# Class scores of a dilated attention: two classes in one contraction, and zero blocks shared

## Chip, cores and metric

The kernel runs on one core of a Trainium2 chip. The metric is the device time of one execution in microseconds; the time before is the median of three runs. Engines are named as in the profile: PE is TensorE's matmul, PEld its weight load, DVE VectorE, ACT ScalarE, POOL GpSimd, SP the engine that issues most of the DMAs.

## What is computed

One encoder block on a sequence of 1024 positions with 1024 channels, in float32: a normalised input is projected to two token mixers and two gates; the mixers are merged by the gates, projected and added to the input; a squared-ReLU MLP and a last norm follow. The part that matters here is the first mixer, attention of 8 heads of 64 dims over three dilations:

```python
DILATED_PATTERNS = ((128, 1), (512, 4), (2048, 16))
def dilated_window_attention(q, k, v):
    for window, dil in DILATED_PATTERNS:
        half = window // (2 * dil)          # 64 in each
        ...                                 # phase split of the sequence by dil, |i-j| <= half in each phase
        outs.append(o); lses.append(lse)
    w = softmax(stack(lses), axis=0)        # the three outputs weighted by their denominators
    return einsum('pbsh,pbshd->bshd', w, stack(outs))
```

The second mixer (4 heads) is a differential attention over all keys; its result goes through `w_branch_b`, times a gate ("branch B" below).

## The kernel before, in words

Positions are kept by class: position t = 4 m + c lies in class c (4 classes) at m (256 places), so dilation 4 and 16 are products inside one class, and dilation 1 is a product of nearby keys of all classes. Float32 operands are split into a high and a low half (`F32R`), and a product is made of several matmuls on halves.

The stages follow each other in the trace: projections and rotary (`rope`, to about 430 us), the differential attention (to about 650 us), the dilated attention with branch B's products as filling (to about 868 us), output projections, MLP. Pools of tiles are opened and closed with the stages, so a stage's first loads need space that the one before gives up. The order of instructions on each engine is worked out when the kernel is built, by a scheduler that goes by the order of the program text and its own estimate of times; engines then run their lists in order.

In `rope`, tile j < 8 holds two heads of the first mixer (queries j < 4, keys 4 to 7). The rotated tile `raw` is split by an ACT copy and a DVE subtract; for j < 4 these write the halves in tile order (8 tiles of 128 queries, each 4 classes x 32). The halves are stored by DMAs on ACT's queue into `qk_d`.

A unit of the dilated stage is one head h and one tile n of 128 queries; 64 units in a row, with values two units (`LAGA`) behind scores. `a_open` loads a head's tiles: `qs` (queries: 64 dims high, 64 dims low on the 128 partitions), `kh` and `kl` (each half of the keys twice, above and below). `a_scores` makes one bank of 128 x 512: class scores in columns 0 to 255 and local scores in 256 to 511. For the class scores each class c has its own weights in `zq`: the queries of the tile with every column outside class c set to zero, so that the four products add up in one 128 x 256 area:

```python
for c in range(NCLS):
    for kk in (o.kh, o.kl):
        nc.tensor.matmul(ps[:, 0:CM], zq[:, n % 4, c, :], kk[:, c * CM:(c + 1) * CM],
```

Eight matmuls, with (high + low) queries on the partitions against high, then low keys. `zq` is filled by one DVE copy for four tiles. Then DVE adds the mask and finds the minimum, ACT takes the exponential, PE transposes, ACT and DVE write the two halves of the transposed weights into `pta` (ten blocks of 128 for each pair of units, two of them zero), and `a_local` and `a_class` multiply by values. After every second head `a_merge` loads shifted sums (`sh`) and denominators (`zr`) from DRAM, POOL adds and multiplies, and `a_split` makes halves on ACT and DVE.

Branch B's products (`branch_b`, 32 steps) are spread over the units as filling; their operand `obT` is loaded by `load_ob`, its weights by `split_weight` (load, ACT copy, POOL subtract; three buffers).

Of the kernel before, what the change touches and what calls it, by code (L numbers as in the profile page):

```python
# [83 lines left out]
def tile_hybrid_block(ctx: ExitStack, tc: tile.TileContext, t: dict, out: bass.AP):  # L84
# [92 lines left out]
    qk_d = [dram(f"qk{j}", [2, P, S]) for j in range(16)]  # L177
    va_d = [dram(f"va{g}", [S, 4, P]) for g in range(2)]
# [309 lines left out]
    def rope(j, raw):  # L488
# [9 lines left out]
        if j < 4:  # L498

            src, to_hi, to_lo = [x.rearrange("p (a b j) -> p a b j", a=a, j=32) for x, a in ((raw, NCLS), (hi, NT), (lo, NT))]  # L500
            to_hi, to_lo = [x.rearrange("p n c j -> p c n j") for x in (to_hi, to_lo)]
        else:
            src, to_hi, to_lo = raw, hi, lo
        nc.scalar.activation(to_hi, src, AF.Copy)
        nc.vector.tensor_tensor(to_lo, src, f(to_hi), op=ALU.subtract)
# [280 lines left out]
    def strided(x, offset, *dims):  # L786

        a = x[:, 0:1]
        return bass.AP(tensor=a.tensor, offset=a.offset + offset, ap=[list(a.ap[0])] + [list(d) for d in dims])
# [29 lines left out]
    def a_values(o, n):  # L819
# [5 lines left out]
        view = [strided(z, 10 * P * pr + P * x, ((4 + 2 * x) * P, 2), (2 * P, 2), (1, P)) for z in pta]  # L825
# [11 lines left out]
    def a_local(o, pr):  # L837
# [13 lines left out]
    def a_class(o):  # L851
        for g in range(2):
            acc = bank1(f"oc{o.h}_{g}", "mm")
            for c in (2 * g, 2 * g + 1):
                oo = acc[:, (c % 2) * CM:(c % 2 + 1) * CM]
                for z in range(2):
                    for kt in range(2):
                        nc.tensor.matmul(oo, o.vc[:, 2 * c + kt, :],
                                         strided(pta[z], 2 * P * kt + 32 * c, (10 * P, 4), (P, 2), (1, 32)),
# [35 lines left out]
    def branch_b():  # L895
        for cp in range(4):
            wh, wl = split_weight(f"wb{cp}", [P, 4, 256],
                                  [(None, w_b[:, 256 * cp:256 * cp + 256].rearrange("(k p) n -> p k n", p=P))], lo="p")
            for u in range(2):
                j = 2 * cp + u  # L900
                c = slice(P * u, P * u + P)
                for h in range(2):
# [3 lines left out]
                    for k in range(4):  # L906
                        for w, z in ((wh, 0), (wh, 1), (wl, 0)):
                            nc.tensor.matmul(acc, w[:, k, c], obT[z][:, k, 512 * h:512 * h + 512],
                                             start=k == 0 and w is wh and z == 0, stop=k == 3 and w is wl)
# [52 lines left out]
    obT = [pob.tile([P, 4, S], F32R, tag=f"ob{z}", name=f"obT{z}") for z in range(2)]  # L962

    def load_ob(j):
        for z in range(2):
            nc.sync.dma_start(f(obT[z])[:, j, :], ob_d[j][z])

    for j in range(3):
        load_ob(j)
# [5 lines left out]
    zqs = [p2a.tile([P, 4, NCLS, P], F32R, tag=f"zq{n}", name=f"zq{n}") for n in range(2)]  # L975


    pta = [p2a.tile([P, 4, 10, P], F32R, tag=f"pta{z}", name=f"pta{z}") for z in range(2)]
    for x in zqs:
        nc.vector.memset(f(x), 0.0)  # L980
    for z in range(2):
        for b in (5, 8):
            nc.gpsimd.memset(f(pta[z])[:, :, b, :], 0.0)
# [6 lines left out]

    LAGA = 2
    for u in range(8 * AH + LAGA):
        h, n = u // 8, u % 8
        if n == 0 and 0 < h < AH - 1:
            ah[h + 1] = a_open(h + 1)
        if h < AH:
# [5 lines left out]
        if u == 7:  # L1002
            load_ob(3)
# [466 lines left out]
```

## Time and profile before

| | |
|---|---|
| median of 3 runs | 1673.32 us (1667.09 to 1675.45) |
| the profiled execution, its own time | 1674.86 us |
| its span, first to last instruction | 1673.1 us |
| mean granted TensorE clock | 0.972 |
| dilated stage, about | 656 to 866 us |

The span is what the trace covers. In a row of the timeline the first number is the start in us from the span's start, the second the duration; in brackets stands how long the engine was idle before and what ended it. Line numbers (L803) are those of the kernel.

### The profile page before, as it was taken

The numbers are of one execution on the slowest core, as the hardware profiler recorded it, in microseconds if no ns is written. First come the engines' busy times: TensorE is split into PE (matmuls) and PEld (weight loads), VectorE is DVE, ScalarE is ACT, GpSimd is POOL, SyncE is SP. The second block draws the span as 40 slices with busy tenths as digits, with TensorE's granted clock in tenths as the row PEclk, the third lists the DMA queues.
The fourth block names the chain that finished last, engine by engine and source line by source line (L and its number), as shares of the span: only waits on it lengthen the run. The fifth ranks groups of instructions, "written<-read, shape, count | busy, mean of one in ns | idle before, by whom it ended". The sixth has DMA issues, their size and how long they took to land. (4 is left out here: it accounts for less than half of the span.)

```text
span 1673.1 us, 20932 instructions
## 1 busy us (share of the span) xinstructions
PE 1557.9 (93%) x7832; PEld 1299.2 (78%) x7832; DVE 1181.4 (71%) x1367; ACT 697.6 (42%) x1064; POOL 585.3 (35%) x289
## 2 busy tenths in 40 slices
PE   8899889988789998989999999899999989999998
PEld 6798667766577887988887878687888867888776
DVE  5976798698688996645547357644355599898984
ACT  4432122232467774544433236444444552333331
POOL 1534444555232332012220003533333344354551
PEclk8999899998999999999999999999999999999999
DMA  6367566555767557656557333444333571423112
GB/s 214 125 210 215 164 196 223 175 184 163 263 194 233 200 191 271 204 180 215 156 162 278 110 130 94 120 128 130 114 101 101 179 268 51 163 74 116 51 38 101
DMA packets 214389, 271.23 MB, mean 162 GB/s; under 512 B 12784, under 2 KB 136848, under 8 KB 214288
## 3 DMA queue, kind: packets, MB, share of 16 engines
q1 hardware_dynamic: 200464, 236.33, 44.4%
q10 hardware_dynamic: 13824, 33.56, 5.3%
q8 instruction: 62, 1.02, 0.3%
q14 instruction: 39, 0.32, 0.1%
HBM read 183.81 MB, written 80.27 MB: 158 GB/s over the span
## 5 line engine op out<-in xcount | busy, mean ns | idle before, releaser
L1359 PE MATMUL p<-b,a 128*128 128x512 f32 x392 | 154.7, 395 | 5.1 <-DVE b L1274 5.1
L1358 PE MATMUL p<-b,a 128*128 128x512 f32 x392 | 154.2, 393 | 3.0 <-ACT a L1273 3.0
L1360 PE MATMUL p<-b,a 128*128 128x512 f32 x392 | 154.4, 396 | 2.0 <-DVE a L1274 1.9
L1274 POOL TENSOR_TENSOR b<-ws,b 128x1024 fp32r<-128x1024 f32 x20 | 61.4, 3088 | 95.3 <-ACT b L1273 85.3
L1359 PEld LDWEIGHTS p<-b,a 128*128 128x128 f32 x392 | 74.2, 189 | 23.0 <-DVE b L1274 6.0
L1274 POOL TENSOR_TENSOR b<-rb,b 128x1024 fp32r<-128x1024 f32 x21 | 70.8, 3390 | 54.7 <-ACT b L1273 46.7
L1360 PEld LDWEIGHTS p<-b,a 128*128 128x128 f32 x392 | 74.0, 189 | 20.1 <-DVE a L1274 3.9
L1358 PEld LDWEIGHTS p<-b,a 128*128 128x128 f32 x392 | 74.1, 189 | 19.8 <-ACT a L1273 3.4
L689 PE MATMUL sb<-kb,qb 128*128 128x512 f32 x256 | 74.7, 416 | 15.1 <-ACT p L694 8.8
L694 ACT ACTIVATE p<-sb,mn 128x1024 f32<-128x1024 f32 x64 | 71.3, 1116 | 38.5 <-DVE mn L692 23.7
L692 DVE TENSOR_REDUCE mn<-sb 128x1 f32<-128x1024 f32 x64 | 76.8, 1217 | 9.7 <-PE sb L689 9.2
L265 DVE TENSOR_TENSOR s<-w 128x512 f32<-128x512 f32 x15 | 16.2, 1081 | 85.8 <-DMA w<-in_w_ff 85.8
L156 POOL TENSOR_SCALAR n_y<-n_ss 128x1 f32<-128x1 f32 x23 | 5.1, 222 | 187.7 <-ACT n_xn L163 183.2
L803 PE MATMUL sa<-kh_a,zq 128*128 128x256 f32 x256 | 68.9, 300 | 1.2 <-DVE mna L812 1.2
L828 DVE TENSOR_TENSOR pta<-ta,pta 128x512 fp32r<-128x512 f32 x64 | 43.8, 688 | 33.9 <-ACT pta L827 33.7
L689 PEld LDWEIGHTS sb<-kb,qb 128*128 128x128 f32 x256 | 45.9, 192 | 27.9 <-ACT p L694 13.1
L1273 ACT ACTIVATE a<-fs 128x1024 fp32r<-128x1024 f32 x28 | 29.4, 1054 | 90.6 <-PE p L1359 71.3
L803 PE MATMUL sa<-kl_a,zq 128*128 128x256 f32 x256 | 65.8, 288 | 0.0
L246 POOL TENSOR_TENSOR wt_f_l<-w,wt_f_h 128x1024 fp32r<-128x1024 f32 x15 | 36.1, 2404 | 83.0 <-ACT wt_f_h L245 70.2
L816 ACT ACTIVATE sm<-sm,mna 128x512 f32<-128x512 f32 x64 | 46.1, 720 | 32.4 <-DVE mna L812 31.8
L827 ACT ACTIVATE pta<-ta 128x512 fp32r<-128x512 f32 x64 | 37.6, 591 | 52.2 <-PE ta L823 44.5
L1145 ACT ACTIVATE c<-c 128x512 f32<-128x512 f32 x64 | 39.9, 624 | 46.6 <-DVE c L292 34.9
(442 smaller groups left out, 4966.4 us busy)
## 6 DMA issues: line engine op xcount, KB each, us to landing
w<-in_w_in SPq DMA_DIRECT2D x32, 512.0 KB, 4.3
qk<-r ACTq DMA_DIRECT2D x32, 512.0 KB, 4.8
f<-c ACTq DMA_DIRECT2D x64, 256.0 KB, 2.0
rb<-in_w_ff SPq DMA_DIRECT2D x32, 512.0 KB, 4.6
ra<-f SPq DMA_DIRECT2D x64, 256.0 KB, 5.0
w<-in_w_ff SPq DMA_DIRECT2D x30, 512.0 KB, 4.2
vb<-vb SPq DMA_DIRECT2D x16, 512.0 KB, 6.6
rot<-raw SPq DMA_DIRECT2D x64, 128.0 KB, 4.5
```

The source lines that it names most:

```text
L689: nc.tensor.matmul(sps[:, 512 * n:512 * n + 512], q[:, z, (qb % 4) * P:(qb % 4 + 1) * P], o.k[m][:, 512 * n:512 * n + 512], start=z == 0, ...
L692: nc.vector.tensor_reduce(mn, sps, axis=AX.X, op=ALU.min)
L694: nc.scalar.activation(p, sps, AF.Exp, scale=-1.0, bias=mn, accum_out=o.zz[qb][:, m:m + 1])
L803: nc.tensor.matmul(ps[:, 0:CM], zq[:, n % 4, c, :], kk[:, c * CM:(c + 1) * CM], start=c == 0 and kk is o.kh, stop=c == NCLS - 1 and kk is ...
L816: nc.scalar.activation(sm, sm, AF.Exp, scale=-1.0, bias=mn, accum_out=stat[h % 2][:, n:n + 1])
L827: nc.scalar.activation(view[0], tv, AF.Copy)
L828: nc.vector.tensor_tensor(view[1], tv, f(view[0]), op=ALU.subtract)
L1145: nc.scalar.activation(c, c, AF.Relu)
L1274: eng.tensor_tensor(lo, x, f(hi), op=ALU.subtract)
L1358: nc.tensor.matmul(acc, ah[:, i % 2, c], bh[:, i % 2, :], start=i == 0 and not more, stop=False, skip_group_check=bool(more))
L1359: nc.tensor.matmul(acc, ah[:, i % 2, c], bl[:, i % 2, :], start=False, stop=False, skip_group_check=bool(more))
L1360: nc.tensor.matmul(acc, al[:, i % 2, c], bh[:, i % 2, :], start=False, stop=last, skip_group_check=bool(more))
```

## The change

The class scores are made for two classes at once: the contraction's 128 partitions hold 64 dims of one class and 64 dims of the next. High and low halves are then separate tiles, and a pair of classes takes three products (high x high, high x low, low x high; low x low is left out), six matmuls in place of eight. For this each head loads its keys (`kp`) and queries (`qp`) once more in a layout by pairs of classes, with queries in natural order from a new store `qn_d`; local scores keep `qs`, `kh` and `kl`. The zero-padded copies become four per four tiles. `pta` has 34 blocks in place of 40: two zero blocks serve all pairs of units, reached by strides. `obT` becomes pieces of half a row, six buffers for each half, and branch B runs over the two halves outermost, so that each weight block is loaded and split twice. The core of the diff:

```diff
+    qn_d = [dram(f"qn{j}", [2, P, S]) for j in range(4)]
...
         if j < 4:
-            src, to_hi, to_lo = [x.rearrange("p (a b j) -> p a b j", a=a, j=32) for x, a in ((raw, NCLS), (hi, NT), (lo, NT))]
-            to_hi, to_lo = [x.rearrange("p n c j -> p c n j") for x in (to_hi, to_lo)]
+            nat = rot.bitcast(F32R), raw.bitcast(F32R)
+            nc.scalar.activation(nat[0], raw, AF.Copy)
+            nc.vector.tensor_tensor(nat[1], raw, f(nat[0]), op=ALU.subtract)
+            for z, x in enumerate((hi, lo)):
+                nc.scalar.dma_start(qn_d[j][z], f(nat[z]))
+                nc.scalar.activation(x.rearrange("p (n c j) -> p c n j", n=NT, j=32),
+                                     f(nat[z]).rearrange("p (c n j) -> p c n j", c=NCLS, j=32), AF.Copy)
         else:
-            src, to_hi, to_lo = raw, hi, lo
-        nc.scalar.activation(to_hi, src, AF.Copy)
-        nc.vector.tensor_tensor(to_lo, src, f(to_hi), op=ALU.subtract)
+            nc.scalar.activation(hi, raw, AF.Copy)
+            nc.vector.tensor_tensor(lo, raw, f(hi), op=ALU.subtract)
...
+    def by_pairs(dst, src):
+        for z in range(2):
+            rows = src[z].rearrange("d (p cc m) -> cc d p m", p=2, cc=2)
+            for cc in range(2):
+                nc.sync.dma_start(f(dst)[64 * cc:64 * cc + 64, z], rows[cc])
+    def a_keys(o):
+        h = o.h
+        o.kp = p2a.tile([P, 2, 2, CM], F32R, tag="kp", name=f"kp{h}", bufs=2)
+        by_pairs(o.kp, qk_d[4 + h // 2][:, 64 * (h % 2):64 * (h % 2) + 64, :])
+    def a_queries(o):
+        h = o.h
+        o.qp = p2a.tile([P, 2, 2, CM], F32, tag="qp", name=f"qp{h}")
+        by_pairs(o.qp.bitcast(F32R), qn_d[h // 2][:, 64 * (h % 2):64 * (h % 2) + 64, :])
...
         if n % 4 == 0:
-            nc.vector.tensor_copy(strided(zq, 0, (512, 4), (160, NCLS), (1, 32)),
-                                  f(o.qs).rearrange("p (n c j) -> p n c j", n=NT, c=NCLS)[:, n:n + 4])
+            for cc in range(2):
+                part = slice(64 * cc, 64 * cc + 64)
+                for z in range(2):
+                    nc.vector.tensor_copy(
+                        strided(zq, 256 * z + 32 * cc, (192, 2), (512, 4), (1, 32), part=part),
+                        strided(o.qp, 512 * z + 32 * n, (CM, 2), (32, 4), (1, 32), part=part))
         ps = bank([P, 512], "s1", f"sa{h}_{n}")
-        for c in range(NCLS):
-            for kk in (o.kh, o.kl):
-                nc.tensor.matmul(ps[:, 0:CM], zq[:, n % 4, c, :], kk[:, c * CM:(c + 1) * CM],
-                                 start=c == 0 and kk is o.kh, stop=c == NCLS - 1 and kk is o.kl)
+        for p in range(2):
+            for zq_, zk in ((0, 0), (0, 1), (1, 0)):
+                nc.tensor.matmul(ps[:, 0:CM], zq[:, n % 4, zq_, p, :], o.kp[:, zk, p, :],
+                                 start=p + zq_ + zk == 0, stop=p + zq_ == 2)
...
-                nc.tensor.matmul(oo, o.vl[:, 2 * pr + a, :], pta[z][:, pr, 4 + 2 * a:6 + 2 * a, :],
+                first = 1 + 8 * pr + 4
+                block, step = ((first, 33 - first), (first + 1, 1), (0, first + 3))[a]
+                nc.tensor.matmul(oo, o.vl[:, 2 * pr + a, :], strided(pta[z], P * block, (P * step, 2), (1, P)),
...
     def branch_b():
-        for cp in range(4):
...
+        for h in range(2):
+            if h:
+                for j in range(2, 4):
+                    load_ob(j, 1)
+            for cp in range(4):
+                wh, wl = split_weight(f"wb{cp}_{h}", [P, 4, 256],
...
+    def load_ob(j, half):
+        obT[j, half] = [pob.tile([P, 512], F32R, tag=f"ob{z}", name=f"obT{z}_{j}_{half}", bufs=6) for z in range(2)]
         for z in range(2):
-            nc.sync.dma_start(f(obT[z])[:, j, :], ob_d[j][z])
+            nc.sync.dma_start(f(obT[j, half][z]), ob_d[j][z][:, 512 * half:512 * half + 512])
...
+    a_queries(ah[0])
+    a_keys(ah[0])
     for u in range(8 * AH + LAGA):
         h, n = u // 8, u % 8
         if n == 0 and 0 < h < AH - 1:
             ah[h + 1] = a_open(h + 1)
+        if n == 0 and h < AH - 1:
+            a_keys(ah[h + 1])
+        if n == 5 and h < AH - 1:
+            a_queries(ah[h + 1])
```

## Rows read from the trace of the kernel before

**Rows 1.** The page's first part: busy time, share of the span, instructions.

```profile
PE 1557.9 (93%) x7832; PEld 1299.2 (78%) x7832; DVE 1181.4 (71%) x1367; ACT 697.6 (42%) x1064; POOL 585.3 (35%) x289
```

**Rows 2.** Windows: length, busy PE, PEld, DVE, ACT, POOL, clock, DMA share, GB/s.

```profile
656.00:866.00 210.00, 196.15 (x1401) 184.13 (x1400) 117.56 (x260) 101.31 (x216) 34.12 (x15) 0.96 0.57 179
680.00:718.00 38.00, 37.98 (x287) 35.87 (x286) 22.90 (x52) 18.26 (x40) 3.27 (x2) 1.00 0.66 202
...
726.00:728.00 2.00, 2.00 (x11) 2.00 (x10) 0.00 (x0) 1.70 (x4) 0.00 (x0) 0.50 0.73 221
```

**Rows 3.** Timeline around the start of the dilated stage, 641 to 669 us.

```profile
641.89 2.53 SPq L966 DMA_DIRECT2D obT<-ob  x4
...
651.75 2.02 SPq L974 DMA_DIRECT2D mask<-in_mask  x1
...
655.04 0.36 DVE L798 CAST zq<-q_a 128x512 fp32r<-128x512 f32 x1
...
666.97 1.28 DVE L760 SCALAR_TENSOR_TENSOR eb<-eb,gsub,rrow 128x1024 f32<-128x1024 f32 x1 [3.15 <-DMA rrow<-rb]
...
668.91 0.80 PE L843 MATMUL ol<-pta,vl 128*128 128x256 f32 x2 [3.20 <-DVE pta L828]
```

**Rows 4.** Timeline of the first merge, 710 to 725 us.

```profile
710.37 0.55 SPq L876 DMA_DIRECT2D zr<-st  x1
...
717.12 2.37 POOL L878 TENSOR_TENSOR sh<-sh,e 64x1024 f32<-64x1024 f32 x1 [17.51 <-DMA zr<-st]
...
721.94 1.06 ACT L888 ACTIVATE oah<-sh 128x1024 fp32r<-128x1024 f32 x1 [7.87 <-POOL sh L879]
...
724.24 1.01 PE L843 MATMUL ol<-pta,vl 128*128 128x256 f32 x3 [5.45 <-ACT pta L827]
```

**Rows 5.** PE's timeline: starts of the score products at two clocks.

```profile
701.14 0.28 PE L803 MATMUL sa<-kh_a,zq 128*128 128x256 f32 x1
...
702.08 0.28 PE L806 MATMUL sa<-kh_a,q_a 128*128 128x256 f32 x1
...
727.18 0.41 PE L803 MATMUL sa<-kh_a,zq 128*128 128x256 f32 x1
...
728.03 0.41 PE L806 MATMUL sa<-kh_a,q_a 128*128 128x256 f32 x1
```

**Rows 6.** Single lines: count, least/median/most ns, first and last start.

```profile
L798 DVE CAST zq<-q_a x16: 362/424/621, 655.0 to 833.0; 128x512 fp32r<-128x512 f32 x16
...
L505 DVE TENSOR_TENSOR r<-raw,r x16: 1214/1226/3421, 180.0 to 422.8; 128x1024 fp32r<-128x1024 f32 x16
...
L150 POOL TENSOR_TENSOR wb_l<-wb_r,wb_h x4: 2372/2402/3186, 617.7 to 731.8; 128x1024 fp32r<-128x1024 f32 x4
```

**Rows 7.** DMA issues over the span: count, KB each, median us to landing.

```profile
qk<-r ACTq DMA_DIRECT2D x32, 512.0 KB, 4.8
...
rot<-raw SPq DMA_DIRECT2D x64, 128.0 KB, 4.5
...
kh_a<-qk SPq DMA_DIRECT2D x8, 512.0 KB, 7.1
...
gb<-gate SPq DMA_DIRECT2D x16, 256.0 KB, 4.0
...
sh<-e SPq DMA_DIRECT2D x8, 256.0 KB, 3.7
```

**Rows 8.** Timeline of the rotary stage's end, 402 to 436 us.

```profile
402.47 1.06 ACT L504 ACTIVATE r<-raw 128x1024 fp32r<-128x1024 f32 x1 [7.11 <-DVE raw L496]
...
406.98 0.33 ACTq L507 DMA_DIRECT2D qk<-r  x1
...
428.00 1.26 SPq L662 DMA_DIRECT2D kb<-qk  x2
...
435.32 1.19 PE L689 MATMUL sb<-kb,qb 128*128 128x512 f32 x2 [6.30 <-DMA qb<-qk]
```

**Rows 9.** SP's waits (total us, times, longest): 405 to 436, 650 to 870 us.

```profile
SPq L662 <- DMA qk<-r: 5.3, 1, 5.3
...
SPq L891 <- ACT oah L888: 10.8, 2, 7.3
```

More of the change, by code (lines that the diff above doesn't have):

```diff
@@ L784, in a_open, with strided @@
         return o
-    def strided(x, offset, *dims):
-        a = x[:, 0:1]
+    def by_pairs(dst, src):
[11 more added lines that the diff above has]
+        by_pairs(o.qp.bitcast(F32R), qn_d[h // 2][:, 64 * (h % 2):64 * (h % 2) + 64, :])
+    def strided(x, offset, *dims, part=slice(0, P)):
+        a = x[part, 0:1]
         return bass.AP(tensor=a.tensor, offset=a.offset + offset, ap=[list(a.ap[0])] + [list(d) for d in dims])
@@ L824, in a_values @@
         pr, x = n // 2, n % 2
-        view = [strided(z, 10 * P * pr + P * x, ((4 + 2 * x) * P, 2), (2 * P, 2), (1, P)) for z in pta]
+        view = [strided(z, P + 8 * P * pr + 2 * P * x, (4 * P, 2), (P, 2), (1, P)) for z in pta]
         tv = tp.rearrange("p (g y) k -> p g y k", g=2)
@@ L858, in a_class @@
                         nc.tensor.matmul(oo, o.vc[:, 2 * c + kt, :],
-                                         strided(pta[z], 2 * P * kt + 32 * c, (10 * P, 4), (P, 2), (1, 32)),
+                                         strided(pta[z], P + P * kt + 32 * c, (8 * P, 4), (2 * P, 2), (1, 32)),
                                          start=kt == 0 and z == 0, stop=kt == 1 and z == 1)
@@ L895, in branch_b @@
     def branch_b():
-        for cp in range(4):
[L897 to L902, printed above, removed]
+        for h in range(2):
[4 more added lines that the diff above has]
+                wh, wl = split_weight(f"wb{cp}_{h}", [P, 4, 256],
+                                      [(None, w_b[:, 256 * cp:256 * cp + 256].rearrange("(k p) n -> p k n", p=P))], lo="p")
+                for u in range(2):
+                    j = 2 * cp + u
+                    c = slice(P * u, P * u + P)
                     g = p2.tile([P, 512], F32, tag="gev", name=f"gb{j}_{h}", bufs=2)
@@ L907, in branch_b @@
                         for w, z in ((wh, 0), (wh, 1), (wl, 0)):
-                            nc.tensor.matmul(acc, w[:, k, c], obT[z][:, k, 512 * h:512 * h + 512],
-                                             start=k == 0 and w is wh and z == 0, stop=k == 3 and w is wl)
+                            nc.tensor.matmul(acc, w[:, k, c], obT[k, h][z], start=k == 0 and w is wh and z == 0, stop=k == 3 and w is wl)
                         if k == 1:
@@ L961, in tile_hybrid_block @@
     pob = obp.__enter__()
-    obT = [pob.tile([P, 4, S], F32R, tag=f"ob{z}", name=f"obT{z}") for z in range(2)]
-    def load_ob(j):
+    obT = {}
+    def load_ob(j, half):
+        obT[j, half] = [pob.tile([P, 512], F32R, tag=f"ob{z}", name=f"obT{z}_{j}_{half}", bufs=6) for z in range(2)]
         for z in range(2):
-            nc.sync.dma_start(f(obT[z])[:, j, :], ob_d[j][z])
+            nc.sync.dma_start(f(obT[j, half][z]), ob_d[j][z][:, 512 * half:512 * half + 512])
     for j in range(3):
-        load_ob(j)
+        load_ob(j, 0)
     s2a = tc.tile_pool(name="s2a", bufs=1, side="right")
@@ L974, in tile_hybrid_block @@
     nc.sync.dma_start(mask, t["mask"])
-    zqs = [p2a.tile([P, 4, NCLS, P], F32R, tag=f"zq{n}", name=f"zq{n}") for n in range(2)]
-    pta = [p2a.tile([P, 4, 10, P], F32R, tag=f"pta{z}", name=f"pta{z}") for z in range(2)]
+    zqs = [p2a.tile([P, 4, 2, 2, P], F32R, tag=f"zq{n}", name=f"zq{n}") for n in range(2)]
+    pta = [p2a.tile([P, 34, P], F32R, tag=f"pta{z}", name=f"pta{z}") for z in range(2)]
     for x in zqs:
@@ L981, in tile_hybrid_block @@
     for z in range(2):
-        for b in (5, 8):
-            nc.gpsimd.memset(f(pta[z])[:, :, b, :], 0.0)
+        for b in (0, 33):
+            nc.gpsimd.memset(f(pta[z])[:, b, :], 0.0)
     branch = branch_b()
@@ L1002, in tile_hybrid_block @@
         if u == 7:
-            load_ob(3)
+            load_ob(3, 0)
+            load_ob(0, 1)
+            load_ob(1, 1)
         if u >= 10 and u % 7 in (0, 2, 4, 6):
```

## The prediction

> **What bounds the kernel now.** I read the page's first part, the windows of the dilated stage, PE's own timeline in it, the waits, and last the timelines around its two ends. TensorE (PE) is busy 93% of the span and no other engine passes 71% [rows 1]. The change acts on the dilated stage, about 656 to 866 us. There PE is busy 196 of 210 us, DVE 118, ACT 101, POOL 34, at a mean granted clock of 0.96, and the DMA engines are 57% busy at 179 GB/s, which is 37.6 MB [rows 2]. In its quiet stretches PE has no gap: 37.98 of 38 us between 680 and 718 at full clock [rows 2]. So the stage is set by PE's list of instructions wherever nothing stalls it. Of the 14 us that PE lacks, 3.2 us end at 668.9 and 5.45 us at 724.24 [rows 3, 4]; behind the second the clock is 0.50 of full, the lower of its two levels [rows 2].
>
> Two things have to be priced: what leaves PE's list, and whether the loads that the new products need make those stalls longer or add others.
>
> **Removed: matmuls.** A unit (one head, 128 queries) issues eight class products before and six after: 64 units, 128 matmuls fewer. What one is worth is not its duration but the distance between starts: eight of them take 701.14 to 702.08, 0.1175 us each, at full clock, and four take 727.18 to 728.03, 0.2125 us each, at half [rows 5]. 128 x 0.1175 = 15.0 us; at the stage's mean clock of 0.96, 15.7 us. The shape (128 rows, 256 columns) stays, so I take 15.7. It can't be more than 128 x 0.2125 = 27.2.
>
> **Added: zero-padded query copies on DVE.** Per four units one copy of 512 elements (median 424 ns) becomes four of 256 on 64 partitions; 16 become 64 [rows 6]. Each lies between half the present one (212 ns) and all of it (424 ns): 13.6 to 27.1 us in place of 6.8, so 7 to 20 us more of DVE. DVE has 92 us idle in the stage [rows 2], and the copies come ahead of only every fourth unit; I cost them at nothing. Without that cover it would be up to 20 us.
>
> What could hold these copies up is POOL: DVE's subtract of two SBUF tiles in the rotary split took 1.23 us at the median and up to 3.42 us, while the present 16 copies never passed 621 ns [rows 6]. [...]
>
> **Added: class keys and queries fetched again from DRAM.** Per head four loads of 128 KB for keys and four for queries, 8 MB in all on 37.6 MB; the four extra weight loads of branch B are 2 MB more. The DMA share goes from 0.57 to about 0.57 x 47.6/37.6 x 210/198 = 0.77, still under one. What counts is lateness, at three places.
>
> (a) *First head.* Before, the first copy starts at 655.04 [rows 3]; its queries were loaded long before. Now queries and keys of head 0 can be fetched only once the space of the stage before is free. The nearest row for that time is the mask load, issued at 651.75 and taking the queue 2.02 us [rows 3]. Eight more issues at 0.55 (zr's) [rows 4] end at 658.2, and with 4.5 us to landing (rot, also 128 KB) [rows 7] the first product would start near 662.7, some 6.6 us later than now. That is the upper bound. Below: the stall ending at 668.91 stood behind a row that DVE waited 3.15 us for [rows 3], and could vanish behind a later start, so the least is -3.2. In favour: the four obT loads at 641.89 [rows 3] halve. I take +2.0.
>
> (b) *Merges.* After every second head its sums are merged through loads from DRAM, and ACT, in order, sits in the split. At the first merge zr is issued at 710.37, POOL starts at 717.12, ACT's split at 721.94, and PE, which needs the copy queued behind it on ACT, resumes at 724.24 after 5.45 us [rows 4]. The key loads of a head (512 KB) are queued in the same stretch; at 179/0.57 = 314 GB/s they hold the engines for 1.7 us. PE also comes to the wait sooner, by the saving of two units, 2 x 0.235 = 0.5 us. Three merges inside the stage: 0 to 6.6 us. This merge is the one whose stall I have a row for, and the keys needn't fall just ahead of zr each time: I take +2.0.
>
> (c) *Queries of later heads.* The query tile has one buffer, so its load goes out only after the copies at a head's fifth unit, and the next head's first products need it four units later, 4 x 2.9 = 11.6 us (198 us over 64 units, less 0.2). Copies (4 x 0.42), issues (4 x 0.55) and landing (4.5 to 7.1 us, rot's and kh_a's) [rows 6, 7] make 8.4 to 11.0. The slack is 0.6 to 3.2 us: I take 0; the cover is those four units, and what it costs if the queue is held up there is rival 2. A load to 64 partitions lands no later than one to 128: sh, 256 KB to 64, 3.7 us; gb, 256 KB to 128, 4.0 us [rows 7]. [...]
>
> **Moved: the rotary split.** For four of the sixteen q/k tiles the halves are made in natural order, stored (2 x 512 KB more), and copied into tile order by two further ACT copies: 8 copies of 1.06 us [rows 8] and 8 issues, on an engine busy 42% of the span [rows 1]. But buffers are held longer, and the end of the stage hangs on them: the next stage's first load waits 5.3 us for the last rotary store [rows 9], goes out at 428.00, and PE starts at 435.32 after 6.30 us idle [rows 8]. The last two tiles of the four are followed by two others that reuse the same pair of store buffers. ACT now has one more copy and an issue between DVE's subtract and the release, 1.06 + 0.33 = 1.4 us [rows 8]; at best 0, at worst a store's landing, 4.8 us [rows 7]. I take 1.4.
>
> **Branch B with the half outermost; zero blocks shared; obT in pieces.** Matmuls and their order within a sum stay. Each weight block is fetched and split twice: 4 x 2.40 us of POOL [rows 6] and 4 ACT copies, with three buffers to run ahead in; POOL idles 176 of 210 us [rows 2]. The value products keep their shapes. Nothing; if a weight came late it would be a load's 4 to 7 us [rows 7] at each of four places.
>
> **Sum.** Against the profiled execution's own 1674.86 us (span 1673.1): -15.7 + 2.0 + 2.0 + 0 + 1.4 = -10.3, so 1664.6. That execution is 1.5 us above the median of the runs, 1673.32, so 1663.0 against the median. About 0.5% (8.4 us) is what a measurement of this kernel can tell from no change; the three runs spread over as much.
>
> **Rivals.**
> 1. *The gain stays in the kernel as waiting.* Start at its bound (6.6), merges at theirs (6.6), rotary end at its (4.8): 18.0 against 15.7, and with any two of the three at the bound the change is inside 0.5%. POOL in DVE's way ends here too: if each of the 16 groups of copies met a POOL instruction as often as POOL is busy, (34 + 9.6)/210 = 0.21, and waited half of 2.40 us, PE would lose up to 4 us, 1667 (0.04 of the chance). For it: both long stalls with a row stand behind a DRAM round trip. Against it: the rows between them show PE without a gap, and the DMA share stays under one. 1665 to 1675, say 1669.
> 2. *Slower: the single query buffer.* SP issues in order, and one store in this stage held it 7.3 us [rows 9]. If the query loads stand behind such a wait, each of seven heads begins with a stall s. At s = 10.3/7 = 1.5 us the forecast is used up; slower by 0.5% begins at (10.3 + 8.4)/7 = 2.7 us. With s = 4 us it is 1663 + 28 = 1691. For it: the slack is 0.6 to 3.2 us, and after a stall the clock can fall. Against it: the 7.3 us wait is one of two, and in the program the query loads come ahead of that store.
> 3. *More than forecast.* The stall at 668.9 goes and nothing is late: -15.7 - 3.2 = -18.9, so 1654.4.
>
> **Chances and range.** Forecast, 1656 to 1665: 0.40. Rival 3: 0.11. Rival 1: 0.38. Rival 2: 0.11. Faster by over 0.5% (below 1665.0) is forecast and rival 3, 0.51; same 0.38; slower 0.11. The range leaves out rival 2 and the far part of rival 3: 1651 to 1680.
>
> **What would show it.** In the profile after: 384 class products, still 0.117 us apart at full clock. (a): how late the first zero-padded copy starts after 655, and what it waits for. (b): PE's gap behind each ACT split. (c): whether the query copy at each head's first unit waits for the load of qp; by more than 2.7 us, and I am wrong. Rotary: the time of the first kb load after 428. DVE busy near all the time between stalls would refute the zero for the copies. If the stage shrinks by 12 us and the total doesn't, the loss is ahead of 656 or in the order that the planner gives the rest.

## The result and the profile after

The changed kernel takes 1686.53 us at the median of five runs, the kernel before beside it 1667.09. The measured ratio is 1.0101, 95% interval 1.0077 to 1.0125 (the two medians alone would give 1.0117). So it is slower by 1.0%, 17 us, where 10 us less were forecast. The profiled execution took 1690.26 us (span 1688.5, mean granted clock 0.967), 15.4 more than the one before.

The first part of the page after, to be held against [rows 1]:

```profile
PE 1554.0 (92%) x7704; PEld 1289.6 (76%) x7704; DVE 1190.1 (70%) x1415; ACT 709.7 (42%) x1076; POOL 588.8 (35%) x293
```

The 128 matmuls are gone from the count, but PE is busy only 4 us less in a span 15 us longer. Where the time went, three rows of PE's instructions by tile show: the first score product of the differential stage (sb), the first class product (sa), the first product of the last merge (ya). The third numbers are the first and last start. First of before, then of after:

```profile
L689 PE MATMUL sb<-kb,qb x256: 387/396/793, 435.3 to 634.0; 128*128 128x512 f32 x128
L803 PE MATMUL sa<-kh_a,zq x256: 277/281/562, 656.1 to 858.2; 128*128 128x256 f32 x128
L1063 PE MATMUL ya<-oaT,wa_h x64: 392/396/792, 868.2 to 917.5; 128*128 128x512 f32 x64
```

```profile
L694 PE MATMUL sb<-kb,qb x256: 387/395/795, 438.8 to 642.0; 128*128 128x512 f32 x128
L829 PE MATMUL sa<-kp,zq x384: 274/282/584, 672.3 to 867.5; 128*128 128x256 f32 x192
L1103 PE MATMUL ya<-oaT,wa_h x64: 392/396/793, 877.4 to 929.2; 128*128 128x512 f32 x64
```

These cut the span into **A** (up to sb, with the rotary at its end), **B** (sb to sa), **C** (sa to ya, the dilated stage) and the rest. From before to after: A 435.3 to 438.8, B 220.8 to 233.5, C 212.1 to 205.1, rest 804.9 to 811.1. The dilated stage did get shorter, by 7 us and not by 14, and more than that was lost ahead of its start. The rest comes from the same program text in every kernel here and took 802.1 to 811.1 us, so its 6 us can't be laid to the change. One execution is a poor yardstick (A of the execution before is 3 us later than in any other kernel with its rotary), so the table at the end of the experiments has A, B and C of all profiles.

A window over the dilated stage after, columns as in [rows 2]. It takes in 12 us ahead of the first class product; the second line is C itself:

```profile
660.00:866.00 206.00, 182.94 (x1241) 165.85 (x1242) 129.98 (x303) 100.66 (x211) 38.81 (x20) 0.94 0.78 230
672.30:877.40 205.10, 188.44 (x1279) 171.09 (x1279) 130.12 (x301) 105.44 (x220) 42.41 (x18) 0.95 0.77 228
```

PE lacks 23 us in the first, 14 in the window before; within C it lacks 16.7 us of 205.1, before 14.8 of 212.1. The DMA share is 0.78 (forecast 0.77). The class products stand as far apart as forecast, 0.118 us at full clock (1.00 granted from 705.2 to 706.4 us):

```profile
705.29 0.87 PE L829 MATMUL sa<-kp,zq 128*128 128x256 f32 x6
706.00 0.28 PE L832 MATMUL sa<-kh_a,q_a 128*128 128x256 f32 x1
```

### The profile page after: what moved, and what is told of

The parts are those of the page before. It is cut to its first block, busy times and chain, and to the rows that moved or that the text cites. A ratio compares the mean times of both kernels' runs of the same rounds, so it can differ in the third digit from the quotient of the medians.

```text
span 1688.5 us, 20827 instructions
## 1 busy us (share of the span) xinstructions
PE 1554.0 (92%) x7704; PEld 1289.6 (76%) x7704; DVE 1190.1 (70%) x1415; ACT 709.7 (42%) x1076; POOL 588.8 (35%) x293
## 4 chain that ended last, share of the span: by engine, by line
PE 54%; DVE 15%; DMA 11%; issue 7%; POOL 6%; ACT 5%; SPq 1%; DVEq 0%; ACTq 0%; POOLq 0%
PE yf L238 5%; PE zf L238 5%; PE p L1399 3%; PE p L1400 3%; PE p L1398 3%; PE 4f L238 2%; PE sa L829 2%; PE yb L939 2%; PE f0f L238 2%; PE f1f L238 2%; PE wo L1158 2%; PE wo L1156 2%; PE wo L1157 2%; PE zq L238 1%; PE sb L694 1%
## 5 line engine op out<-in xcount | busy, mean ns | idle before, releaser
L1314 POOL TENSOR_TENSOR b<-rb,b 128x1024 fp32r<-128x1024 f32 x21 | 63.9, 3058 | 64.8 <-ACT b L1313 64.8
L829 PE MATMUL sa<-kp,zq 128*128 128x256 f32 x384 | 66.7, 305 | 12.2 <-DMA kp<-qk 5.8
L829 PEld LDWEIGHTS sa<-kp,zq 128*128 128x128 f32 x384 | 55.9, 202 | 16.6 <-DVE zq L823 12.7
L496 POOL TENSOR_TENSOR raw<-raw,cos_t 128x1024 f32<-128x1024 f32 x16 | 44.5, 2785 | 37.1 <-DMA rot<-raw 34.8
```

Source lines behind the costliest of these rows:

```text
L496: nc.gpsimd.tensor_tensor(raw, raw, cos_t, op=ALU.mult)
L829: nc.tensor.matmul(ps[:, 0:CM], zq[:, n % 4, zq_, p, :], o.kp[:, zk, p, :], start=p + zq_ + zk == 0, stop=p + zq_ == 2)
L1314: eng.tensor_tensor(lo, x, f(hi), op=ALU.subtract)
```

## Experiments

Where a diff cuts code down, "+" stands against the kernel that the heading names. Each edit also lets the scheduler order the engines' lists anew; no run holds that order fixed, so a part of any one difference may be the order.

### The rotary: e8 and e10 on the kernel before

e8 puts the new rotary alone into the kernel before; e10 does so without the two stores.

```diff
+            nat = rot.bitcast(F32R), raw.bitcast(F32R)
+            nc.scalar.activation(nat[0], raw, AF.Copy)
+            nc.vector.tensor_tensor(nat[1], raw, f(nat[0]), op=ALU.subtract)
+            for z, x in enumerate((hi, lo)):
+                nc.scalar.dma_start(qn_d[j][z], f(nat[z]))      # not in e10
+                nc.scalar.activation(<x in tile order>, <nat[z]>, AF.Copy)
```

e8: 

> The kernel before with the new rotary alone: natural-order halves in the rotary's two buffers, their stores, and the tile-order copies from them; nothing reads the new stores, and everything after is as before. Theory A: 7 to 12 us above the kernel before, 1674 to 1680. Rival (the rotary costs this only together with the rest, through the planner's order): within 2 us, about 1668.

e10: 

> The kernel before with the new rotary, but without the natural-order stores: the halves are still made in the rotary's two buffers and copied into tile order. All outputs are computed (nothing here reads those stores). Theory A (the stores hold the buffers): within 3 us of the kernel before, 1668 to 1673. Rival (the longer chain of copies on ScalarE delays the buffers and the weight splits): 6 to 9 us above it, as with the stores.

Measured: e8 1678.90 us, ratio 1.0062 (1.0038 to 1.0087); e10 1670.96, 1.0016 (0.9998 to 1.0033). Both lie where theory A put them, 0.46% apart (7.7 us). With the stores A is 443.6, without them 431.2. The waits between 270 and 440 us (total, times, longest) name the chain. In the changed kernel:

```profile
POOL raw L496 <- DMA rot<-raw: 32.8, 7, 10.9
...
PE f0q L238 <- ACT wa_q_h L246: 4.5, 1, 4.5
...
PE f0q L238 <- POOL wa_q_l L247: 4.3, 1, 4.3
...
PE yq L238 <- POOL ws_q_l L247: 4.2, 1, 4.2
```

In e10:

```profile
POOL raw L496 <- DMA rot<-raw: 12.1, 5, 4.7
...
PE yq L238 <- POOL ws_q_l L247: 3.2, 2, 1.8
...
PE f0q L238 <- POOL wa_q_l L247: 1.3, 1, 1.3
```

Why the rotation loads are late, SP's own waits in the changed kernel (300 to 440 us) tell, and the timeline what stands behind them:

```profile
SPq L494 <- DMA qn<-rot: 16.5, 4, 8.0
```

```profile
341.42 0.33 ACTq L505 DMA_DIRECT2D qn<-raw  x1
...
344.94 3.39 POOL L496 TENSOR_TENSOR raw<-raw,cos_t 128x1024 f32<-128x1024 f32 x1 [10.90 <-DMA rot<-raw]
...
348.29 2.34 POOL L247 TENSOR_TENSOR wa_q_l<-w,wa_q_h 128x1024 fp32r<-128x1024 f32 x1
...
350.69 0.79 PE L238 MATMUL f0q<-hB,wa_q_l 128*128 128x512 f32 x1 [4.27 <-POOL wa_q_l L247]
```

A natural half lies in the buffer of `rot`, and the next tile's `rot` load must wait until its store has landed (SP: 16.5 us over four loads). POOL stood idle for 10.90 us before its multiply of 344.94, until that load had landed, and came to the split of a weight only behind it, at 348.29; PE waited 4.27 us for that split. Theory A holds.

### The start and the swapped query tile: e1, e2

e1 undoes the rotary and fills the query tile from the tile-order store, halves swapped. The resident query tile has its high and low rows interleaved, which the copies of this run don't follow, so they pair other rows than they should; the copies and matmuls are those of the changed kernel in number and shape, and a head's query loads are two of 256 KB in place of four of 128 KB.

```diff
-        o.qp = p2a.tile([P, 2, 2, CM], F32, tag="qp", ...)
-        by_pairs(o.qp.bitcast(F32R), qn_d[...])
+        o.qp = p2a.tile([P, S], F32, tag="qp", ...)
+        for z in range(2):
+            nc.sync.dma_start(o.qp[64 - 64 * z:128 - 64 * z], qk_d[h // 2][z][64 * (h % 2):64 * (h % 2) + 64, :])
```

> The rotary part is as in the kernel before: no natural-order stores, copies in the old order. The query tile for the zero-padded operand is filled by two loads of 64 rows each from the tile-order store, the halves swapped, and each copy reads it or the resident query tile; all outputs are computed as in the changed kernel. Theory A (the natural-order stores hold the rotary's two buffers, the next rotation loads come late, and a POOL multiply that waits for them holds up the weight splits behind it): the rotary part loses its 7 us of extra stalls and some of the 3 us lost in the first 40 us of the differential stage, so 7 to 10 us less than the changed kernel, about 1677 to 1680 us. Rival (the rotary's difference is a difference between two executions or of the planner's order): no change beyond 2 us, about 1685.

Measured: 1673.10 us, ratio 1.0025 (1.0002 to 1.0047), A 429.5: a little below the forecast. The rotary is worth what e8 says, seen from the other side; C (201.6) is 4 us shorter too, which the theory did not have.

e2 keeps all of the changed kernel but the place of the first loads:

```diff
-        o.kp = p2a.tile([P, 2, 2, CM], F32R, tag="kp", ..., bufs=2)
+        o.kp = (p2a if h % 2 else p2).tile([P, 2, 2, CM], F32R, tag=f"kp{h % 2}", ...)   # head 0: loaded at step 28
...
+    a_queries(ah[0])          # ahead of the mask
     nc.sync.dma_start(mask, t["mask"])
-        if n == 0 and h < AH - 1:
+        if n == (2 if h == 0 else 0) and h < AH - 1:
             a_keys(ah[h + 1])
```

> The changed kernel with the first head's paired keys loaded during the differential stage into a buffer of their own, its queries first in the queue when the space is free, ahead of the mask, and the second head's keys two steps later. Theory B (the dilated stage starts 8 us late because its first operands stand in the queue behind the mask and beside the second head's keys): the first class product comes 6 to 8 us sooner, about 1679 us. Rival (the loads start when the space of the stage before is free, whatever their order, or the wait only moves on to the next product): less than 2 us, about 1685.

Measured: 1684.29 us, ratio 1.0095 (1.0079 to 1.0111): the rival's time, no clear gain on the changed kernel. B is 227.9, 6 us less than there. From the last product of the stage before (ob) to the first class product it takes 8.8 us; in the changed kernel 13.1, in the five kernels with the old operands 5.3 by the mean. So half of what the start lost stays. First the start in the changed kernel, to be held against [rows 3]:

```profile
660.75 1.86 SPq L1006 DMA_DIRECT2D mask<-in_mask  x1
...
662.65 2.51 SPq L796 DMA_DIRECT2D qp<-qn  x4
...
665.21 6.78 SPq L796 DMA_DIRECT2D kp<-qk  x8
...
669.43 2.17 DVE L823 CAST zq<-qp 64x256 fp32r<-64x256 f32 x8 [2.34 <-DMA qp<-qn]
...
672.26 0.77 PE L829 MATMUL sa<-kp,zq 128*128 128x256 f32 x2 [5.49 <-DMA kp<-qk]
```

Twelve issues follow the mask, four of them for head 1's keys, and PE waits for the last of head 0's. In e2 the keys are there, but the queries still go out when the space is free, and the copies and the product then stand behind the normalisation of the stage before, whose row PE transposes first:

```profile
661.06 3.04 SPq L796 DMA_DIRECT2D qp<-qn  x4
...
666.94 0.47 PE L613 MATMUL row_nb<-ident,stat 128*128 128x128 f32 x1 [2.35 <-DVE stat L757]
...
667.66 2.08 DVE L823 CAST zq<-qp 64x256 fp32r<-64x256 f32 x8
...
668.51 2.31 PE L829 MATMUL sa<-kp,zq 128*128 128x256 f32 x8 [1.09 <-DVE zq L823]
```

What theory B says of the keys holds; its forecast does not, for with one operand early the wait moves on to the queries, the copies and the normalisation, as the rival had it. With both early (e14 below) the same distance is 5.2 us.

### Parts of the change on the kernel before: e3, e4

e3 takes over `pta`, `obT` and branch B word for word and leaves the class products as before; e4 only shortens the loop:

```diff
-        for c in range(NCLS):
+        for c in range(NCLS - 1):
```

e3: 

> The kernel before with only the shared zero blocks, the halved tiles of branch B's input and branch B with the half outermost (its weights split eight times in place of four). Class scores and rotary as before. Theory C (these are hidden): within 2 us of the kernel before, about 1667. Rival (the second split of the weights and its loads cost what the dilated stage shows in small stalls): 3 to 6 us above it, about 1671.

e4: 

> The kernel before with the class scores made of the first three classes' products, six matmuls in place of eight; the fourth class is left out of the scores, so the output is not the reference's. Nothing is loaded or copied beyond the kernel before. Theory D (the dilated stage is bound by TensorE, and the matmuls taken out come off its length one for one): 13 to 16 us below the kernel before, about 1652 us. Rival (the stage waits for its softmax chain and its loads, and the saved time turns into waiting): 0 to 5 us below.

Measured: e3 1667.65 us, ratio 0.9984 (0.9970 to 0.9999), so these parts cost nothing. e4 1657.56, 0.9934 (0.9914 to 0.9954), C 198.4: 11 us by the ratio, the same by C against the mean 209.1 of four profiles with the old products. That is less than theory D's 13 to 16: most of the matmuls' time comes off the stage when nothing is added to it, and a part turns into waiting even there.

### Copies and loads in the changed kernel: e6, e7, e9, e17, e18

```diff
-        if n % 4 == 0:                                  # e6: copies for head 0 only
+        if n % 4 == 0 and h == 0:
-            a_keys(ah[h + 1]) ... a_queries(ah[h + 1])  # e7: loads for head 0 only
+            ah[h + 1].kp, ah[h + 1].qp = ah[h].kp, ah[h].qp
+        if n == 2: a_pad(ah[h], 4)                      # e9: copies two steps ahead,
+        if n == 6: a_pad(ah[h + 1], 0)                  #     query loads at n == 3
-                    nc.vector.tensor_copy(              # e17
+                    nc.scalar.copy(
-        o.qp = p2a.tile(..., tag="qp", ...)             # e18
+        o.qp = p2a.tile(..., tag="qp", ..., bufs=2)
```

e6: 

> The changed kernel with the copies into the zero-padded tiles made for head 0 alone; the other heads reuse them, so the scores of heads 1 to 7 are not the reference's. Loads stay. Theory E (the 64 small copies, queued on VectorE and held behind POOL, are what keeps TensorE waiting within the dilated stage): 5 to 9 us below the changed kernel, 1677 to 1681. Rival (VectorE is off the path; the small waits come from the loads or the softmax chain): within 2 us, about 1685.

e7: 

> The changed kernel with the paired keys and queries loaded for head 0 alone; the other heads use head 0's, so their scores are not the reference's. Copies stay. Theory F (the 56 further loads fill the one DMA queue and delay the weights, gates and shifted halves behind them): 3 to 6 us below the changed kernel, 1680 to 1683. Rival (they are hidden): within 2 us, about 1685.

e9: 

> The changed kernel with the same 64 copies, each group made two steps ahead of the product that reads it (the zero-padded tile is free by then), and the next head's queries loaded two steps sooner for it; all outputs are computed. Theory E (the 17 us that went with the copies were waits at the point of use: a group of four copies stands between two tiles' products, behind whatever VectorE does there): 6 to 12 us below the changed kernel, 1674 to 1680. Rival (the copies' own time on VectorE, or VectorE held by POOL, is the price, wherever they stand): less than 3 us, about 1685.

e17: 

> The changed kernel with its 64 copies on ScalarE in place of VectorE, nothing else; all outputs are computed. Theory G (in the changed kernel too the dilated stage's loss is the copies' place in VectorE's queue): 5 to 10 us below the changed kernel, 1676 to 1681. Rival (the loss comes from the copies and loads being chained to each other, whichever engine copies): within 2 us, about 1685.

e18: 

> The changed kernel with two buffers for the loaded queries in place of one (the small row tile of the normalisation has one in place of two, for the space); all outputs are computed. Rival 2 of the prediction (the single query buffer holds the queue or the copies up at each head): 4 to 9 us below the changed kernel, 1677 to 1682. Against it (no wait of the queue stands before these loads in the trace): within 2 us, about 1685.

Measured ratios to the kernel before, the changed kernel's being 1.0101: e6 0.9998 (0.9980 to 1.0017), e7 1.0015 (0.9997 to 1.0033), e9 1.0082 (1.0060 to 1.0104), e17 1.0051 (1.0030 to 1.0072), e18 1.0054 (1.0035 to 1.0073). C, 205.1 to 207.1 with the changed products as they are (after, e2, e9), is 193.1, 196.5, 207.1, 199.5, 200.9. e6 and e7 gave back far more than forecast (17 and 14 us by the ratios). So copies and loads each hold the stage; taking out either brings back most of it, and the effects don't add. Bytes alone are not the cause: e6 still makes the loads, and its window shows a DMA share as high as the changed kernel's, with PE lacking 9.5 us in 191:

```profile
667.00:858.00 191.00, 181.46 (x1274) 167.62 (x1274) 111.21 (x244) 102.58 (x218) 35.88 (x15) 0.97 0.80 235
```

Of the 13 us between 206 and 193 PE's waits name 5.6 (changed kernel, 672 to 878 us):

```profile
PE sa L829 <- DVE zq L823: 5.6, 4, 2.9
```

C of e6, to be held against the second window of the section on the result, shows why the waits name so little. PE lacks 10.4 us there in place of 16.7, and for the same 1279 matmuls it is busy 182.7 us in place of 188.4, at a granted clock of 0.97 in place of 0.95. About half of what came back was PE's busy time and not its idle time:

```profile
666.60:859.70 193.10, 182.73 (x1279) 168.70 (x1280) 112.20 (x245) 103.10 (x218) 36.98 (x16) 0.97 0.80 236
```

e9 shows that with one query buffer moving the copies in the program doesn't free them: theory E falls for the changed kernel (the same move took 17.5 us off C in e12 below, and in e16 it comes with two query buffers). e17 shows that VectorE as their engine is half of the cost (theory G), e18 that the single query buffer, rival 2 of the prediction, costs 5 us of C, against my note that no wait of the queue stood before these loads. For the space e18 also takes one of the two buffers of a small row tile away, which no run takes apart.

### Loads in pieces of 64 rows: e5, e11, e12

e5 joins e1 and e2 and stacks the halves of the resident tiles; e11 makes each stacked load as two; e12 adds e9's copies.

```diff
-        q_src = qk_d[jq][:, r, :].rearrange("z d s -> d z s")
+        q_src = qk_d[jq][:, r, :]                                  # e5; keys likewise, [0, 2] outermost
+            for a in range(2):                                     # e11, e12
+                nc.sync.dma_start(f(x)[64 * a:64 * a + 64], src[a][r, :])
```

e5: 

> The edits of the first two runs together, and head 0's swapped query tile in a resident buffer too, so that both operands of the first class product are loaded during the differential stage. The resident queries and keys of the dilated heads are loaded with the two halves stacked and not interleaved, as the swapped tile needs; all outputs are computed. Theory A+B: the rotary is as in the first run (about 1673 us), and the first class product loses 8 of the 13 us that separate it there from branch B's first matmul: 1664 to 1667 us, at or a little below the kernel before. Rival (the start moves its wait on to the normalisation of the stage before or to the next products, as the second run's 2 us suggests): 1671 to 1674.

e11: 

> The fifth run's kernel with every stacked load made as two loads of 64 rows; all outputs are computed. Theory (one load over two blocks of 64 rows was what cost 200 us): 1664 to 1668 us if the earlier first operands give back 6 us of the start, 1671 to 1674 if the start only moves its wait on.

e12: 

> The kernel of the run above with the copies made two steps ahead; all outputs are computed. If the three causes add up (rotary, first operands, copies at the point of use): 1656 to 1662 us, 0.4 to 0.8% below the kernel before, most of the 15 us that the removed matmuls are worth. Rival (the small waits of the dilated stage pass from one cause to the next): 1665 to 1670, no faster than before.

Measured: e5 1876.39 us, ratio 1.1235 (1.1208 to 1.1262); e11 1703.05, 1.0211 (1.0180 to 1.0242); e12 1691.45, 1.0143 (1.0125 to 1.0161). In e11 A (429.3) and B (222.0) are back at the kernel before's, as expected of A+B, and C is 247.0. All three forecasts missed, for a cause that I had built in: the form of the loads. In e12 the copies ahead take C back to 229.5. By tile, the third load of a head in e1 and in e5, where the numbers are the time that SP needed to issue it:

```profile
L601 SPq DMA_DIRECT2D kl_a<-qk x8: 513/550/597, 602.6 to 800.7; - x8
```

```profile
L601 SPq DMA_DIRECT2D kl_a<-qk x8: 515/8090/10736, 614.9 to 975.3; - x8
```

The same 512 KB keep the queue for 8 us at the median when the two halves are the outermost dimension, while the two loads of that form just ahead of them take 0.54 and 0.51 us (e5, 760.40 and 761.04 us); what holds the third, no run shows. The window of e5's dilated stage has a DMA share of 0.43, and PE is busy 172 of its 300 us:

```profile
760.00:1060.00 300.00, 172.44 (x1015) 153.24 (x1014) 103.30 (x236) 82.94 (x171) 40.40 (x17) 0.76 0.43 131
```

e11 repairs that (each of the two pieces takes 0.59 us at the median) and still is 45 us longer in C than e1, which differs in C by its three loads of 128 rows for each head (and, at its start, by head 0's and head 1's operands coming later, and by head 0's swapped queries not taking one of the eight buffers that the resident tiles share). The windows of e1 and e11:

```profile
662.00:860.00 198.00, 185.84 (x1268) 168.14 (x1268) 133.59 (x300) 105.83 (x220) 42.29 (x18) 0.97 0.80 234
```

```profile
655.00:890.00 235.00, 197.87 (x1225) 174.28 (x1225) 129.39 (x295) 102.62 (x216) 40.24 (x17) 0.88 0.77 203
```

By these rows the DMA engines would move an estimated 234/0.80 = 292 GB/s at full share in e1 and 203/0.77 = 264 in e11.

### The causes mended together: e13 to e16

e13 stores the rotated query once, before its split, and leaves the rotary as it was; the split happens in the copies. e14 loads head 0's operands early, e15 moves the high copies to ScalarE, e16 makes the copies two steps ahead.

```diff
+            nc.scalar.dma_start(qn_d[j], raw)                                       # rope, j < 4
+        o.qp = p2a.tile([P, 2, CM], F32, tag="qp", ..., bufs=2)                      # two loads of 128 KB
+                nc.vector.tensor_copy(hi, src)       # e15, e16: nc.scalar.activation(hi, src, AF.Copy)
+                nc.vector.tensor_tensor(lo, src, f(hi), op=ALU.subtract)
```

e13: 

> The changed kernel with one natural-order store of the rotated queries, before their split, in place of two after it; the rotary's halves and copies as in the kernel before. The zero-padded tile's high half is copied from the loaded query, its low half is the difference (a tensor_tensor), so two loads of 128 KB for each head in place of four, in two buffers. All outputs are computed. Theory: the rotary gives back its 8 us (the loaded buffers are free as before), and with half the query loads and copies that take the place of 32 of the 64, 2 to 6 us of the dilated stage: 1672 to 1677. Rival (the dilated stage's loss hangs on the keys' loads or the number of copies, which stay): 1678.

e14: 

> The run above with head 0's queries and the even heads' paired keys in the space that both stages share, loaded during the differential stage, and the second head's keys two steps later. Theory: the start gives back 7 to 8 us as it did in the eleventh run: 1664 to 1669, about the kernel before. Rival (the wait moves into the first head): 1671 or more.

e15: 

> The run above with the 32 copies of the high halves on ScalarE in place of VectorE. Theory G (what is left of the dilated stage's loss is VectorE's queue and its copies that stand still while POOL works): 3 to 7 us below the run above, 1659 to 1664, below the kernel before. Rival (the loads, or ScalarE as the new place of the same wait): no change, or up to 4 us above.

e16: 

> The run above with the copies made two steps ahead of the product that reads them. Theory: with two query buffers the copies can really go ahead, and the product waits for none: 2 to 4 us below the run above. Rival (the planner had placed them early enough): the same within 1.5 us.

Measured: 1670.70 us, ratio 0.9994 (0.9978 to 1.0010); 1666.22, 0.9973 (0.9954 to 0.9992); 1662.34, 0.9952 (0.9933 to 0.9972); 1657.72, 0.9927 (0.9901 to 0.9952). e16 computes everything and beats both kernels: 0.7% below the one before. One step by itself (e13 to e14, e14 to e15, e15 to e16: 0.2% each) is within the noise of the ratios; what they show is the sum of the three, 0.67%. In e14 the first copy and product follow the mask at once, with no load to wait for:

```profile
651.82 1.89 SPq L1010 DMA_DIRECT2D mask<-in_mask  x1
...
654.75 0.54 DVE L826 CAST zq<-qp 64x256 fp32r<-64x256 f32 x2
...
655.34 0.75 PE L831 MATMUL sa<-kp,zq 128*128 128x256 f32 x4 [0.30 <-DVE zq L826]
```

Its C is still 204.7, and the timeline shows one reason:

```profile
743.90 2.37 POOL L907 TENSOR_TENSOR sh<-sh,e 64x1024 f32<-64x1024 f32 x1 [20.05 <-DVE pta L856]
744.30 2.12 DVE L826 CAST zq<-qp 64x256 fp32r<-64x256 f32 x1
...
746.35 0.67 DVE L856 TENSOR_TENSOR pta<-ta,pta 128x512 fp32r<-128x512 f32 x1
...
747.08 0.50 PE L873 MATMUL ol<-pta,vl 128*128 128x256 f32 x2 [1.59 <-DVE pta L856]
```

POOL's addition is at work until 746.27, and the copy, 0.29 us by its median, ends at 746.42; DVE's next subtract and PE wait behind it. With the high copies on ScalarE (e15) C falls to 199.6, and e16's PE waits for no copy any more. Copies by tile in e14 and in e15 (least, median, most ns):

```profile
L826 DVE CAST zq<-qp x32: 222/291/2430, 654.7 to 830.1; 64x256 fp32r<-64x256 f32 x32
```

```profile
L826 ACT ACTIVATE zq<-qp x32: 399/414/422, 653.1 to 821.1; 64x256 fp32r<-64x256 f32 x32
```

### All profiles

A, B, C in us, worked out from the rows by tile as above, one execution of each kernel; the ratio is that to the kernel before. The four kernels with the old class products and the old dilated loads differ by 5 us in C, so a few us in one row tell little.

| kernel | ratio | A | B | C |
|---|---|---|---|---|
| before | 1 | 435.3 | 220.8 | 212.1 |
| after | 1.0101 | 438.8 | 233.5 | 205.1 |
| e1 rotary undone, swapped tile | 1.0025 | 429.5 | 230.8 | 201.6 |
| e2 keys of head 0 early | 1.0095 | 440.6 | 227.9 | 206.2 |
| e3 blocks alone | 0.9984 | 429.4 | 220.2 | 206.8 |
| e4 six products alone | 0.9934 | 432.1 | 221.4 | 198.4 |
| e5 stacked loads | 1.1235 | 428.6 | 284.8 | 351.9 |
| e6 no copies | 0.9998 | 435.5 | 231.1 | 193.1 |
| e7 no loads | 1.0015 | 438.8 | 230.3 | 196.5 |
| e8 rotary alone | 1.0062 | 443.6 | 222.8 | 208.3 |
| e9 copies ahead | 1.0082 | 439.8 | 232.0 | 207.1 |
| e10 rotary, no stores | 1.0016 | 431.2 | 221.7 | 209.0 |
| e11 64-row loads, early | 1.0211 | 429.3 | 222.0 | 247.0 |
| e12 the same, copies ahead | 1.0143 | 430.3 | 222.3 | 229.5 |
| e13 one store | 0.9994 | 433.4 | 225.0 | 205.8 |
| e14 and early operands | 0.9973 | 437.1 | 218.2 | 204.7 |
| e15 and copies on ScalarE | 0.9952 | 434.1 | 221.2 | 199.6 |
| e16 and copies ahead | 0.9927 | 434.3 | 218.8 | 198.1 |
| e17 copies on ScalarE | 1.0051 | 441.3 | 228.1 | 199.5 |
| e18 two query buffers | 1.0054 | 441.0 | 226.7 | 200.9 |

## Why the prediction was wrong

By means over the table the change costs: in A 439.9 (eight kernels with the new rotary and its stores) against 430.6 (seven with the old one), +9.3; in B 230.4 (the seven with late first operands: after, e1, e6, e7, e9, e17, e18) against 221.4 (before, e3, e4, e8, e10), +9.0; in C 206.1 (after, e2, e9) against 209.1 (before, e3, e8, e10), -3.0. Together +15.3; the ratio says +17.

**The matmuls, -15.7: the price of one was right, the sum was nearer to 11.** The products stand 0.118 us apart, as priced [rows 5]. With the products cut and nothing added (e4) C is 10.7 below the mean of before. With the copies gone (e6) it is 193.1, 16.0 below, but there the old copies and the stall of [rows 3] are gone too.

**The copies "at nothing", and the queries of later heads, 0: the step that failed most.** I counted DVE's idle time in the stage and the slack of the loads, each by itself. (The slack was also summed wrong: 198 us over 64 units has the saving in it already, so four units are 12.4 us and the slack 1.4 to 4.0, which makes the 0 look safer still.) But C keeps 3 of its 16 us (and the 3 of the stall below are lost with them). Without the copies 13 us come back, without the loads 9.6, on ScalarE 6.6, with a second query buffer 5.2. I read this as a chain of load, copy and product with little room in it. VectorE idles 75 of the 205.1 us of C in the changed kernel, and PE still waits 5.6 us for its copies: idle time is cover only if it lies where the copy is wanted. How these shares overlap, and why a second buffer helps when no wait of the queue was named, stays open: PE's waits name 5.6 us of the 13, and half of the 13 is PE's own busy time, at a lower clock for a part of it.

**First head, +2.0: mis-sized.** The upper bound was 6.6. The runs show 9.0 in B, of which 7.7 lie between the last product of the stage before and the first class product (13.0 by the mean of the seven, 5.3 of the five). The mechanism was right and the bound nearly so: from the mask's issue to the first product it had 10.95 us, the profile after has 672.26 - 660.75 = 11.5. I took a value near the lower end because a stall that followed [rows 3] might vanish. It did (DVE's product with `rrow`, at 682.41 after, has no wait before it), but that is 3 us off C, and the start still cost a little over its bound. That head 1's keys would stand between head 0's in the queue I had not priced.

**Rotary, +1.4: wrong place.** I priced the end of the stage and the last two tiles, and the buffers of the stores; the cost is 9.3 us in its middle, where the buffers of the natural halves wait for their stores and POOL, which waits 32.8 us for the loads into them, comes late to the weight splits. The bound of 4.8 was for one landing; here several follow each other (SP waits 16.5 us over four loads). e13's single store gives only a part back: A of e13 to e16 is 434.7 by the mean, 5 below the kernels with both stores and 4 above those with none.

**Merges, +2.0: not paid.** At the first merge after, PE waits 2.4 us and not 5.45 as in [rows 4], and no later merge in C makes it wait so for `pta`:

```profile
733.85 1.06 ACT L916 ACTIVATE oah<-sh 128x1024 fp32r<-128x1024 f32 x1 [2.75 <-POOL sh L907]
...
735.44 0.99 PE L871 MATMUL ol<-pta,vl 128*128 128x256 f32 x3 [2.44 <-ACT pta L853]
```

**Branch B and the zero blocks, 0: right** (e3).

**The rivals.** Rival 1 had the right idea, gain turned into waiting, and its places (start, rotary) but not the sizes, and the merges did not pay; rival 2, the one with the right sign, names a part of C's loss (e18) and not the bulk of the total. POOL in DVE's way, costed at up to 4 us, is real: two of the 64 copies after, both begun while POOL was at work, took 1.6 and 2.4 us where the median is 0.286, and in e14 the case above is one of several (two copies from 711.34 on take 4.17 us together).

## What to carry to other kernels

When a change replaces work on the bound engine by loads and copies, follow each new load and copy to the first instruction that waits for it, at the start of the stage and at each later repeat; a free share of an engine or of the DMA says little about that. Here a store from a buffer that was about to be reused held up the next load into it, and with it unrelated work that came behind that load's user (32.8 us of POOL's waits with the stores, 12.1 without): store less, and from a buffer with room, as e13 does from `raw` (four buffers, `rot` has two). When the form of a load is changed, look at its issue time in the queue's own rows (0.55 us against 8.09 in e5).

## What the hardware showed that I had not expected

- The third load of a head, its outermost dimension two, held SP for 8.09 us at the median (up to 10.7, e5) where the same bytes with the halves interleaved took 0.55 (e1).
- Loads of 64 rows: C grew from 201.6 to 247.0 when the three resident tiles of a head came as six such loads, and the estimated rate at full DMA share fell from 292 to 264 GB/s. The prediction had read from two landings that loads to 64 partitions land no later [rows 7]; in e11 the pieces of `kh_a` landed after 8.8 us at the median and those of `q_a` after 4.3, in e1 the whole loads, of twice the bytes, after 6.3 and 5.3. What part of the 45 us the 64 rows explain no run here separates.
- A VectorE copy of 0.29 us took 2.12 us beside a POOL addition that had begun 0.40 us earlier, and ended 0.15 us after it. The subtracts of the rotary split in the kernel before show the same: the eight of 16 that began while a POOL instruction was at work took 2.03 to 3.42 us, the eight others 1.21 to 1.23. On ScalarE (e15) the same copy never took more than 0.422 us.
